# Attention values projected last and transposed one block at a time; attention operands fetched through GpSimd's DMA queue

## The chip, the cores and the metric

The kernel runs on one core of a Trainium2 chip. The core has five engines that run their own instruction streams in order: TensorE (PE in the profile), VectorE (DVE), ScalarE (ACT), GpSimd (POOL) and SyncE (SP, which only issues transfers here). They meet at semaphores. The metric is the device time of one execution in microseconds; less is better. The kernel before takes 1205.3 us as the median of three runs (1205.23 to 1207.03).

## The reference

One layer of a decoder with two token mixers beside each other, on 1024 tokens of width 1024 in float32. Cut to what matters:

```python
h = rmsnorm(x, norm_g)
proj = h @ w_in                       # 1024 x 9232, all projections at once
# four heads of gated linear attention (GLA), chunks of 64 tokens, a recurrent state per head
o_gla = gla_chunked(g_q, g_k, g_v, log_a)
y_a = (rmsnorm(o_gla, gla_norm_g) * silu(g_gate)) @ w_pa
# eight heads of stick-breaking attention, head width 128, blocks of 128 queries
z = q @ k.T * scale                   # strictly causal
A = exp(log_sigmoid(z) + (sum over s<j<t of log_sigmoid(-z)))
y_b = ((A @ v) * silu(s_gate)) @ w_pb
gates = sigmoid(m_logits + b_gate)
out = rmsnorm(x + (gates[0] * y_a + gates[1] * y_b) @ w_o, final_g)
```

## The kernel before, in words

**Precision.** Every large product is done in three passes: each float32 operand is split into a high part (an ACT copy into the matmul type, line 165) and a low part (a DVE subtraction, line 166), and high x high, high x low and low x high are added in PSUM. So each projected weight or operand costs ACT, DVE and PE work in step.

**The pairs.** Most projections are done two 128-column blocks at a time by a seven-product scheme (class Pairs, lines 62 to 99, and `pair_job`). A pair is seven units, u0 to u6; each unit is 12 matmuls of 128x512 (lines 270 to 272). Units 1, 4, 5 and 6 each finish one 128x512 block of the result, which is then evicted. While a unit of one pair runs, the weights of the next are split (lines 165 and 166), and GpSimd forms four weight differences per pair (lines 244 to 247). There are 28 pairs: three merge-gate pairs, the eight of GLA, the stick-breaking queries, values and keys in turn (four times query, value, key), four merge-gate pairs of the second branch, and one last merge-gate pair.

**The value pairs.** Queries and keys are evicted as they are. A value block is needed with tokens on the partitions, and as differences of neighbouring tokens. So the eviction of a value block copies the ends of its 128-token blocks into `vend` (line 605), forms the differences on DVE (lines 613, 615, 617), and appends a function `turn` to the list `late`: four PE transposes into a PSUM bank named tr (line 622), the split of that bank (lines 165 and 166), and two stores into `d_v` (line 626). `Pairs.run` takes the list as it stands before a unit and runs all of it behind that unit's product. Unit 5 leaves two functions there (its own block and the held one of unit 4), units 1 and 6 leave one each. There are two tr banks; GLA's transposes (lines 830 and 870) use the same two.

**GLA beside the pairs.** From about 280 us to 718 us the 32 GLA steps run, each with four units of the pairs between its parts. Its chain goes over PE, ACT, DVE, one small GpSimd power (line 231) and back. In this stretch the order on the engines is set by a scheduler, which places instructions by its own estimates.

**The attention.** From 737 us to about 1012 us the 64 stick-breaking steps run (8 heads x 8 blocks of 128 queries). A step is scores on PE (lines 966 to 968), a sigmoid on ACT (969), a scan on DVE (972), transposes on PE (984), and twice a head the product with the values (1005 to 1007). Between them stand filler units, 24 matmuls each (lines 204 to 206): first the attention's output gates, later the GLA branch's output projection, whose results are multiplied by a merge gate fetched from `d_ga` (line 590) and passed through a sigmoid (591). `load_head` fetches the keys (1 MB, line 909) and the two halves of the values (512 KB each, line 912) of a head; `load_q` fetches two query blocks (256 KB, line 919) into one of two buffers, which comes free when PE has used the queries before. All of it goes through SP's queue, as do every other load and nearly every store: an SP instruction whose buffer isn't free holds up all that stand behind it.

Of the kernel before, what the change touches and what calls it, by code (L numbers as in the profile page):

```python
# [9 lines left out]
F32 = mybir.dt.float32  # L10
# [14 lines left out]
DV = 256  # L25
# [5 lines left out]
C_SQ, C_SK, C_SV, C_SG, C_MA, C_MB = 3088, 4112, 5136, 6160, 7184, 8208  # L31
# [37 lines left out]
class Pairs:  # L69
# [13 lines left out]
    def run(self, n=None):  # L83
        while self.at < 7 * len(self.jobs) and (n is None or n > 0):
            i, u = divmod(self.at, 7)
            nxt = self.jobs[i + 1] if i + 1 < len(self.jobs) else None
            if u == 0:
                self.jobs[i]["split"][3]()
            elif nxt and u in (2, 4, 6):
                nxt["split"][u // 2 - 1]()  # L90
            if u == 1 and i + 2 < len(self.jobs):
                self.jobs[i + 2]["load"]()
            due = self.late[:]
            self.late.clear()
            self.jobs[i]["unit"](u)
            for f in due:
                f()
            self.at += 1
            if n is not None:
                n -= 1  # L100
# [3 lines left out]
def hybrid_layer(ctx: ExitStack, tc: tile.TileContext, x, norm_g, w_in, w_up, b_dec,  # L104
# [5 lines left out]
    nc = tc.nc  # L110
# [386 lines left out]
    f = {}  # L497
# [44 lines left out]
    def qk_pair(c0, i, dst):  # L542
        def evict(J, n, bank, add):
            v = total(bank, add)
            o = stage()
            split(v, o[:, 0], o[:, 1])
            nc.sync.dma_start(dst[2 * i + J][:, :, half(n)], o.bitcast(F32))

        return pair_job(w_in, c0 + i * DV, evict)
# [27 lines left out]
    def merge_pair(c0, i, dst):  # L577
        def evict(J, n, bank, add):
            if add is None:
                add = ev.tile([P, HALF], F32, tag="f", name="f")  # L580
                nc.scalar.activation(add, bank, AF.Copy)
            else:
                total(bank, add)
            nc.sync.dma_start(dst[2 * i + J][:, half(n)], add)

        return pair_job(w_in, c0 + i * DV, evict)
# [6 lines left out]
    def sv_pair(i):  # L593


        held = []

        def evict(J, n, bank, add):
            if add is None:
                add = ev.tile([P, HALF], F32, tag="f", name="f")  # L600
                nc.scalar.activation(add, bank, AF.Copy)
            else:
                total(bank, add)
            h = 2 * i + J
            nc.vector.tensor_copy(vend[:, h, 4 * n:4 * n + 4], add[:, P - 1:HALF:P])
            held.append((J, n, h, add))
            if (J, n) != (1, 1):
                while held:
                    diff(*held.pop())

        def diff(J, n, h, add):
            d = ev.tile([P, HALF], F32, tag="f", name="f")
            nc.vector.tensor_sub(d[:, 1:HALF], add[:, 0:HALF - 1], add[:, 1:HALF])
            if n:
                nc.vector.tensor_sub(d[:, 0:1], vend[:, h, 3:4], add[:, 0:1])
            else:
                nc.vector.tensor_scalar(d[:, 0:1], add[:, 0:1], -1.0, None, op0=ALU.mult)

            def turn():
                pt = ps.tile([P, HALF], F32, tag="tr", name="tr")  # L620
                for b in range(4):
                    nc.tensor.transpose(pt[:, b * P:(b + 1) * P], d[:, b * P:(b + 1) * P], ident)
                o = stage()
                split(pt, o[:, 0], o[:, 1])
                for e in range(2):
                    nc.sync.dma_start(d_v[h][:, 4 * n:4 * n + 4, e],
                                      o[:, e].bitcast(F32).rearrange("p (b c) -> p b c", c=P))

            late.append(turn)

        return pair_job(w_in, C_SV + i * DV, evict)

    def gla_qk(i):
# [5 lines left out]
    late = []  # L639
    pairs = Pairs([merge_pair(C_MA, i, d_ga) for i in range(3)] +  # L640
                  gla_qk(0) + [gg_pair(0), gg_pair(1)] + gla_qk(1) + [gg_pair(2), gg_pair(3)] +
                  [f for i in range(4) for f in (qk_pair(C_SQ, i, d_q), sv_pair(i), qk_pair(C_SK, i, d_k))] +
                  [merge_pair(C_MB, i, d_gb) for i in range(4)] + [merge_pair(C_MA, 3, d_ga)], late)

    dq_ctx = ExitStack()
    dq = dq_ctx.enter_context(tc.tile_pool(name="dq", bufs=1, reuse_waits="tile"))
# [259 lines left out]

    def load_head(h):
        kts[h] = sl.tile([P, 2, T], F32R, tag="k", name="k")
        nc.sync.dma_start(kts[h].bitcast(F32), d_k[h])
        vts[h] = [sl.tile([P, NT // 2, 2, P], F32R, tag="v", name="v", bufs=3) for _ in range(2)]  # L910
        for i, v in enumerate(vts[h]):
            nc.sync.dma_start(v.bitcast(F32), d_v[h][:, 4 * i:4 * i + 4])

    def load_q(h, m):

        tag = "d" + "hl"[m % 2]
        t = sw.tile([P, 4, P], F32R, tag=tag, name="q", bufs=1).rearrange("p a c -> p (a c)")
        t = t.rearrange("p (s c) -> p s c", s=2)
        nc.sync.dma_start(t.bitcast(F32), d_q[h][:, :, m * DV:(m + 1) * DV])
        for e in range(2):  # L920
            qts[h, 2 * m + e] = t[:, :, e * P:(e + 1) * P]

# [568 lines left out]
```

## Time and profile before

The profiled execution took 1206.26 us and its span is 1204.4 us; the three runs have a median of 1205.3 us.

| | busy us (share of the span) |
|---|---|
| PE (matmul) | 1184.0 (98%) |
| PEld (weight load) | 996.3 (83%) |
| DVE | 823.4 (68%) |
| ACT | 522.1 (43%) |
| POOL | 281.4 (23%) |

| stage, us from the span's start | what runs |
|---|---|
| 0 to 114 | norm, transposes of x, GLA values |
| 114 to 726 | the 28 pairs; GLA steps beside them from about 280 |
| 737 to 1012 | attention, with filler projections |
| 1044 to 1204 | output projections of the second branch, then the output |

Such a profile is read by the engine that is never idle: PE is busy in 98% of the span, at the full granted clock in all 40 slices of the page. An engine's idle time matters only where PE waits for it.

### The profile page before, as it was taken

The page shows a single profiled execution, that of the slowest core. Times are in us where ns is not written, and L with a number is a line of the kernel's source. Part 1 is how long each engine was busy: PE and PEld are TensorE (multiplying, and loading weights), DVE is VectorE, ACT ScalarE, POOL GpSimd, SP SyncE. Part 2 cuts the span into 40 slices and gives each one's busy share as a digit, 9 for nine tenths or more (in the row PEclk, how much of TensorE's full clock was granted, in tenths as well). Part 3 has the DMA queues.
Part 4 walks back from the last instruction along what each step waited for, and adds up shares of the span by engine and source line. Part 5 has one row for each costly group of instructions (what it writes and reads, how often), then busy time and mean ns, then how long its engine had stood idle before and what let it go on. Part 6 is the DMA issues. An engine that isn't in the chain of part 4 may idle for free.

```text
span 1204.4 us, 17022 instructions
## 1 busy us (share of the span) xinstructions
PE 1184.0 (98%) x6087; PEld 996.3 (83%) x6087; DVE 823.4 (68%) x1373; ACT 522.1 (43%) x985; POOL 281.4 (23%) x237
## 2 busy tenths in 40 slices
PE   8999999999999999999999999999999999999997
PEld 8999878788888887878788887888888888888886
DVE  6474877886777777766665544665675765578986
ACT  5343662333444444445443433343443443455543
POOL 1495523242424222322422300000000000800001
PEclk9999999999999999999999999999999999999999
DMA  7443449997556656656654359554689537748652
GB/s 282 193 152 130 149 168 304 324 328 241 163 161 186 220 177 201 205 179 201 206 175 141 126 184 294 187 192 156 235 282 314 176 123 249 253 163 287 219 192 105
DMA packets 192496, 247.65 MB, mean 206 GB/s; under 512 B 12406, under 2 KB 125068, under 8 KB 190876
## 3 DMA queue, kind: packets, MB, share of 16 engines
q1 hardware_dynamic: 191836, 245.52, 61.2%
q8 instruction: 48, 0.79, 0.3%
q10 hardware_dynamic: 576, 1.05, 0.2%
q14 instruction: 36, 0.29, 0.1%
HBM read 154.25 MB, written 92.27 MB: 205 GB/s over the span
## 4 chain that ended last, share of the span: by engine, by line
PE 85%; DVE 5%; DMA 3%; ACT 3%; issue 2%; POOL 1%; SPq 0%; ACTq 0%; DVEq 0%
PE pp L270 13%; PE pp L271 12%; PE pp L272 12%; PE pp L223 8%; PE pp L204 5%; PE pp L206 5%; PE pp L205 5%; PE z L966 2%; PE av L1006 1%; PE av L1007 1%; PE av L1005 1%; PE tr L984 1%; PE z L967 1%; PE z L968 1%; PE xb L1375 1%
## 5 line engine op out<-in xcount | busy, mean ns | idle before, releaser
L166 DVE TENSOR_TENSOR wl<-tt,wh 128x1024 fp32r<-128x1024 f32 x56 | 69.7, 1244 | 43.4 <-ACT wh L165 43.2
L972 DVE TENSOR_TENSOR_SCAN be<-be,m 128x128 f32<-128x128 f32 (+3 forms) x64 | 86.1, 1350 | 10.3 <-ACT be L969 10.0
L309 DVE TENSOR_TENSOR f<-pp,f 128x512 f32<-128x512 f32 x84 | 57.6, 686 | 51.1 <-PE pp L272 49.2
L244 POOL TENSOR_TENSOR tt<-raw 128x512 f32<-128x512 f32 x28 | 41.6, 1487 | 204.0 <-DVE wl L166 179.0
L166 DVE TENSOR_TENSOR wl<-raw,wh 128x1024 fp32r<-128x1024 f32 x47 | 65.2, 1389 | 31.3 <-ACT wh L165 30.7
L165 ACT ACTIVATE wh<-tt 128x1024 fp32r<-128x1024 f32 x56 | 59.2, 1058 | 61.7 <-PE pp L271 61.2
L165 ACT ACTIVATE wh<-raw 128x1024 fp32r<-128x1024 f32 x47 | 49.6, 1058 | 83.0 <-PE pp L205 41.3
L276 ACT ACTIVATE f<-pp 128x512 f32<-128x512 f32 x84 | 49.5, 591 | 71.3 <-PE pp L272 71.3
L1158 POOL TENSOR_TENSOR N<-A,A 128x512 f32<-128x512 f32 x4 | 6.6, 1649 | 304.0 <-DMA A<-d_osb 304.0
L231 POOL TENSOR_TENSOR r<-r,nhalf 128x1 f32<-128x1 f32 x40 | 24.7, 617 | 187.9 <-DVE r L230 177.4
L969 ACT ACTIVATE be<-z 128x384 f32<-128x384 f32 (+4 forms) x96 | 46.6, 494 | 49.8 <-PE z L968 48.7
L270 PE MATMUL pp<-ha22h,wh 128*128 128x512 f32 x112 | 44.5, 397 | 1.4 <-DVE f L309 1.4
L270 PE MATMUL pp<-S3h,wh 128*128 128x512 f32 x112 | 44.3, 395 | 1.5 <-ACT f L276 1.5
L270 PE MATMUL pp<-ha11h,wh 128*128 128x512 f32 x112 | 44.6, 398 | 0.0
L270 PE MATMUL pp<-S1h,wh 128*128 128x512 f32 x112 | 44.3, 396 | 0.0
L270 PE MATMUL pp<-ha12h,wh 128*128 128x512 f32 x112 | 44.2, 395 | 0.0
L270 PE MATMUL pp<-S2h,wh 128*128 128x512 f32 x112 | 44.0, 392 | 0.0
L270 PE MATMUL pp<-S4h,dh 128*128 128x512 f32 x112 | 43.9, 392 | 0.0
L272 PE MATMUL pp<-ha11h,wl 128*128 128x512 f32 x112 | 43.9, 392 | 0.0
L272 PE MATMUL pp<-ha12h,wl 128*128 128x512 f32 x112 | 43.7, 391 | 0.0
L272 PE MATMUL pp<-ha22h,wl 128*128 128x512 f32 x112 | 43.7, 390 | 0.0
L271 PE MATMUL pp<-ha22l,wh 128*128 128x512 f32 x112 | 43.7, 390 | 0.0
(519 smaller groups left out, 3902.6 us busy)
## 6 DMA issues: line engine op xcount, KB each, us to landing
raw<-in_w_in_dram SPq DMA_DIRECT2D x31, 1024.0 KB, 6.1
d_gv<-o SPq DMA_DIRECT2D x16, 512.0 KB, 2.6
d_t<-t SPq DMA_DIRECT2D x16, 512.0 KB, 5.8
v<-d_gv SPq DMA_DIRECT2D x32, 256.0 KB, 3.1
d_ogl<-o SPq DMA_DIRECT2D x64, 128.0 KB, 2.4
d_q<-o SPq DMA_DIRECT2D x16, 512.0 KB, 3.8
d_v<-o SPq DMA_DIRECT2D x32, 256.0 KB, 2.4
d_k<-o SPq DMA_DIRECT2D x16, 512.0 KB, 4.0
```

The lines of the kernel that those rows point to most:

```text
L165: nc.scalar.activation(hi, src, AF.Copy)
L166: eng.tensor_sub(lo, src, hi.bitcast(F32))
L204: nc.tensor.matmul(pt, whi[:, kb], h_, start=kb == 0, stop=False)
L205: nc.tensor.matmul(pt, whi[:, kb], l_, start=False, stop=False)
L206: nc.tensor.matmul(pt, wlo[:, kb], h_, start=False, stop=kb == KB - 1)
L223: nc.tensor.matmul(pt[:, 0:n], *ops[kb][i], start=k == 0, stop=k == 3 * KB - 1)
L270: nc.tensor.matmul(pt, bh[:, j], ah[:, j], start=first and j == 0, stop=False, skip_group_check=True)
L271: nc.tensor.matmul(pt, bh[:, j], al[:, j], start=False, stop=False, skip_group_check=True)
L272: nc.tensor.matmul(pt, bl[:, j], ah[:, j], start=False, stop=j == 3, skip_group_check=True)
L276: nc.scalar.activation(t[nm], t[bank], AF.Copy)
L309: nc.vector.tensor_add(add, bank, add)
L972: nc.vector.tensor_tensor_scan(rest, rest, m1[:, off:T][:, ::-1], 1.0, op0=ALU.mult, op1=ALU.max)
```

## The change

Three things. First, `Pairs.run` takes one function of `late` per unit and leaves the rest for the units behind it, where it took all. Second, the four value pairs no longer stand between the query and key pairs: queries and keys alternate, then come the four merge-gate pairs, then the four value pairs in a row, then the last merge-gate pair. Third, the loads of keys, values and queries of the attention are issued by GpSimd, not by SP.

```diff
@@ Pairs.run
-            due = self.late[:]
-            self.late.clear()
+            due = self.late.pop(0) if self.late else None
             self.jobs[i]["unit"](u)
-            for f in due:
-                f()
+            if due:
+                due()
@@ the list of pairs
-                  [f for i in range(4) for f in (qk_pair(C_SQ, i, d_q), sv_pair(i), qk_pair(C_SK, i, d_k))] +
-                  [merge_pair(C_MB, i, d_gb) for i in range(4)] + [merge_pair(C_MA, 3, d_ga)], late)
+                  [f for i in range(4) for f in (qk_pair(C_SQ, i, d_q), qk_pair(C_SK, i, d_k))] +
+                  [merge_pair(C_MB, i, d_gb) for i in range(4)] +
+                  [sv_pair(i) for i in range(4)] + [merge_pair(C_MA, 3, d_ga)], late)
@@ load_head, load_q
-        nc.sync.dma_start(kts[h].bitcast(F32), d_k[h])
+        nc.gpsimd.dma_start(kts[h].bitcast(F32), d_k[h])
...
-            nc.sync.dma_start(v.bitcast(F32), d_v[h][:, 4 * i:4 * i + 4])
+            nc.gpsimd.dma_start(v.bitcast(F32), d_v[h][:, 4 * i:4 * i + 4])
...
-        nc.sync.dma_start(t.bitcast(F32), d_q[h][:, :, m * DV:(m + 1) * DV])
+        nc.gpsimd.dma_start(t.bitcast(F32), d_q[h][:, :, m * DV:(m + 1) * DV])
```

Lines 97 to 640 of the kernel before have numbers lower by one in the changed kernel (622 becomes 621), so the rows below differ in these numbers too.

**DVE at the end of a value pair.** Before, here the second value pair (o<-tr,o is the low half of a turned block, vend and f<-f its differences):

```order
L613 TENSOR_TENSOR f<-f 128x511
L615 TENSOR_TENSOR f<-vend,f 128x1
L166 TENSOR_TENSOR wl<-tt,wh 128x1024
L605 COPY vend<-f 128x4
L613 TENSOR_TENSOR f<-f 128x511
L615 TENSOR_TENSOR f<-vend,f 128x1
L166 TENSOR_TENSOR o<-tr,o 128x512 x3
L309 TENSOR_TENSOR f<-pp,f 128x512
```

Changed, between the first and the second value pair:

```order
L612 TENSOR_TENSOR f<-f 128x511
L614 TENSOR_TENSOR f<-vend,f 128x1
L165 TENSOR_TENSOR o<-tr,o 128x512 x2
L308 TENSOR_TENSOR f<-pp,f 128x512
...
L604 COPY vend<-f 128x4
L612 TENSOR_TENSOR f<-f 128x511
L616 TENSOR_SCALAR f<-f 128x1
L165 TENSOR_TENSOR o<-tr,o 128x512
```

Three low halves in a row have become two, and the third stands behind the first eviction of the next pair, which is a value pair as well and brings its own copy and differences with it.

**SP where the second half of the filler projections begins** (oa22l is the last of the GLA results fetched, d_ga a merge gate, v and q values and queries, d_osb and d_ma results). Before:

```order
L1077 DMA oa22l<-d_ogl_141 128x4x512
L912 DMA v<-d_v_97 128x1024
L590 DMA o<-d_ga_142 128x512
L919 DMA q<-d_q_81 128x2x256
L1012 DMA d_osb_112<-f 128x512
L912 DMA v<-d_v_98 128x1024
L919 DMA q<-d_q_81 128x2x256
L1052 DMA d_ma_158<-o 128x512
L590 DMA o<-d_ga_143 128x512
```

Changed:

```order
L1077 DMA oa22l<-d_ogl_141 128x4x512
L589 DMA o<-d_ga_142 128x512
L589 DMA o<-d_ga_143 128x512
L589 DMA o<-d_ga_144 128x512
L1012 DMA d_osb_112<-f 128x512
```

The first merge gate stands directly behind oa22l, and the second and third follow it.

**PE at the start of the attention**, the rows ahead of the scores of the fifth query block (z 128x320, which needs the third query load; tr<-ident,be is a turned block, pp a filler). Before:

```order
L204 MATMUL pp<-ha11h,wh 128x512
L205 MATMUL pp<-ha11l,wh 128x512
L206 MATMUL pp<-ha11h,wl 128x512
L984 MATMUL tr<-ident,be 128x128 x3
L204 MATMUL pp<-ha12h,wh 128x512
L205 MATMUL pp<-ha12l,wh 128x512
L206 MATMUL pp<-ha12h,wl 128x512
L204 MATMUL pp<-ha11h,wh 128x512
L205 MATMUL pp<-ha11l,wh 128x512
L966 MATMUL z<-k,q 128x320
```

Changed:

```order
L967 MATMUL z<-k,q 128x512
L968 MATMUL z<-k,q 128x512
L204 MATMUL pp<-ha12l,wh 128x512
L984 MATMUL tr<-ident,be 128x128
L205 MATMUL pp<-ha12h,wl 128x512
L984 MATMUL tr<-ident,be 128x128 x2
L966 MATMUL z<-k,q 128x320
```

Between the scores of the second block and these scores stood 14 fillers and 6 transposes; now there are 6 fillers and 3 transposes, and the others stand behind. On POOL, which has no other work from 722 us on but for the loads, this third query load stands behind the clearing of the buffers for the scan, the second head's keys and the first half of its values.

## The prediction

> **What bounds the kernel now.** I read the engines' busy time first, then what PE waited for, then each wait in order of time. The page's first row and the waits of PE (line, releaser: us in total, times, longest):
>
> ```profile
> PE 1184.0 (98%) x6087; PEld 996.3 (83%) x6087; DVE 823.4 (68%) x1373; ACT 522.1 (43%) x985; POOL 281.4 (23%) x237
> PE tr L622 <- DVE o L166: 2.1, 2, 1.1
> PE z L966 <- ACT be L969: 1.3, 1, 1.3
> PE tr L622 <- DVE f L617: 0.9, 2, 0.6
> PE tr L870 <- DVE o L166: 0.8, 1, 0.8
> PE tr L984 <- DVE atl L166: 0.7, 1, 0.7
> PE z L966 <- DMA q<-d_q: 0.2, 1, 0.2
> ```
>
> PE sets the time, and the change takes no matmul away. So it can win only the idle time of PE in the stages that it touches, and these six rows are all of it: 2.1 + 1.3 + 0.9 + 0.8 + 0.7 + 0.2 = 6.0 us. The same waits in the timeline of PE (start, duration, instruction, idle time before it and its releaser):
>
> ```profile
> 439.17 0.66 PE L622 MATMUL tr<-ident,f 128*128 128x128 f32 x4 [0.58 <-DVE f L617]
> 457.33 0.66 PE L622 MATMUL tr<-ident,f 128*128 128x128 f32 x4 [1.02 <-DVE o L166]
> 527.00 0.66 PE L622 MATMUL tr<-ident,f 128*128 128x128 f32 x4 [1.06 <-DVE o L166]
> 597.07 0.44 PE L870 MATMUL tr<-ident,on 128*128 128x128 f32 x2 [0.81 <-DVE o L166]
> 742.58 0.55 PE L984 MATMUL tr<-ident,be 128*128 128x128 f32 x3 [0.70 <-DVE atl L166]
> 744.46 0.41 PE L966 MATMUL z<-k,q 128*128 128x320 f32 x1 [0.18 <-DMA q<-d_q]
> 926.18 0.38 PE L966 MATMUL z<-k,q 128*128 128x256 f32 x1 [1.26 <-ACT be L969]
> ```
>
> Three groups: the turned value blocks (439 to 597), the start of the attention (742 to 744), and one wait for ACT in its middle (926).
>
> **Part 1, one block per product.** The waits at 457, 527 and 597 (2.9 us) are for "DVE o", the low half taken from a tr bank. There are two such banks. A 128x512 matmul takes PE 0.23 us, as a row of the chain of waits has it:
>
> ```profile
> 737.93 0.23 PE pp L204
> ```
>
> Before, two blocks are turned behind unit 6 and a third behind unit 0 of the next pair, so the third needs a bank that was filled only one unit earlier. Now it is the third unit in a row with one block each, and the bank it needs was filled two units earlier. That is one more product, about 2.7 us (12 matmuls), against a longest wait of 1.06. I count all 2.9 us as gone. The two waits for "DVE f L617" (0.9 us) stand behind unit 2, where the first block of a pair is turned one unit after its difference, before and now; I keep them. Bounds for this part without the next one: -3.8 to 0.
>
> **Part 2, value pairs in a row.** The work is the same, but DVE's load is no longer mixed. Windows of one pair each, a value pair and two merge-gate pairs (length, PE, PEld, DVE, ACT, POOL busy, granted clock, DMA share, GB/s), and what a value pair alone asks of DVE, the groups of all four (busy us, mean ns):
>
> ```profile
> 428.35:453.29 24.94, 24.36 (x129) 19.94 (x128) 18.81 (x44) 10.75 (x24) 6.43 (x6) 1.00 0.54 166
> 639.83:662.73 22.90, 22.90 (x118) 18.89 (x116) 12.66 (x32) 9.28 (x22) 6.17 (x6) 1.00 0.43 137
> 662.73:685.43 22.70, 22.70 (x116) 18.71 (x114) 12.01 (x25) 9.43 (x18) 5.86 (x6) 1.00 0.42 136
> L613 DVE TENSOR_TENSOR f<-f 128x511 f32<-128x511 f32 x16 | 10.8, 681 | 0.0
> L166 DVE TENSOR_TENSOR o<-tr,o 128x512 fp32r<-128x512 f32 x16 | 10.6, 679 | 1.4 <-ACT o L165 1.4
> L605 DVE COPY vend<-f 128x4 f32<-128x4 f32 x16 | 4.5, 281 | 0.2
> L615 DVE TENSOR_TENSOR f<-vend,f 128x1 f32<-128x1 f32 x8 | 4.5, 559 | 0.0
> L617 DVE TENSOR_SCALAR f<-f 128x1 f32<-128x1 f32 x8 | 1.2, 144 | 0.0
> 370.45 0.44 PE tr L622 x4
> ```
>
> A merge-gate pair has 12.3 us of DVE in 22.8 us. A value pair adds 31.6 / 4 = 7.9 us of DVE, and 4 x 0.44 = 1.8 us of PE: in a row, DVE is busy 20.2 of 24.6 us, 82%. Before, a third of that spilled into a key pair. As long as DVE may idle less than 4.4 us in such a pair, PE hides it: cost 0. If it can't, this cover is gone, and PE waits for differences and banks (rival D). GpSimd's and SP's work per pair is the same.
>
> **Part 3, loads through GpSimd.** Nothing is saved on the DMA engines; what moves is which queue a late load holds up. Two places count.
>
> At 908 us SP fetches the first merge gate. The rows of SP, then of ACT, then of what ACT waited for in all:
>
> ```profile
> 900.42 1.06 SPq L1077 DMA_DIRECT2D oa22l<-d_ogl  x1
> 908.26 0.33 SPq L912 DMA_DIRECT2D v<-d_v  x1
> 908.64 0.42 SPq L590 DMA_DIRECT2D o<-d_ga  x1
> 914.00 0.72 ACT L591 ACTIVATE o<-o,vcol 128x512 f32<-128x512 f32 x1 [2.09 <-DMA o<-d_ga]
> 924.93 0.72 ACT L591 ACTIVATE o<-o,vcol 128x512 f32<-128x512 f32 x1 [2.06 <-DMA o<-d_ga]
> 925.55 1.06 ACT L969 ACTIVATE be<-z 128x512 f32<-128x512 f32 x2
> ACT o L591 <- DMA o<-d_ga: 34.8, 11, 10.9
> ```
>
> SP stood from 901.5 to 908.26 at a value load whose buffer wasn't free, with the merge gate behind it. It landed late, ACT stood 2.09 us, the result's store and with it the reuse of the buffers came late, ACT stood 2.06 us once more at 924.93, and the sigmoid behind it (925.55) is what PE waits for at 926.18. Now the load stands directly behind oa22l, 6.7 us earlier. Its chain moves up by ACT's first wait, 2.09 us, more than PE's 1.26: -1.3. The other bound is 0, if a later merge gate, which still waits for a store, is late instead.
>
> At the start of the attention the third query load has the shortest time between the release of its buffer and its use. Rows of PE, SP and the chain of waits, and the landing of all 32 query loads:
>
> ```profile
> 737.65 0.28 PE L968 MATMUL z<-k,q 128*128 128x256 f32 x1
> 738.65 0.32 SPq L571 DMA_DIRECT2D d_sg<-o  x1
> 739.08 0.52 SPq L919 DMA_DIRECT2D q<-d_q  x1
> 739.08 5.34 DMA q<-d_q
> L919 SPq DMA_DIRECT2D q<-d_q x32: 523/524/878, 728.2 to 979.7; - x32
> DMA to landing us min/median/max: 2.9/4.4/7.3
> ```
>
> The buffer is free at 737.65 + 0.28 = 737.9; SP, busy with a store, issued at 739.1. GpSimd has nothing to do there and issues about 738.1. But PE's order changed too: the scores that need this load have moved ahead of 8 fillers and 3 transposes. PE was ready for them at 744.46 - 0.18 = 744.3; without 8 x 0.23 and 3 x 0.11 us and without the wait of 0.70 at 742.58 it is ready at 744.3 - 2.9 = 741.4. The load lands between 738.1 + 2.9 = 741.0 and 738.1 + 7.3 = 745.4. I take the duration that this very load had, 5.34, since no row shows a load through GpSimd: 743.4, so PE waits 2.0 us where it waited 0.70 + 0.18: +1.1. Bounds -0.9 to +3.1. In the notes called the Trainium skill, the page "DMA: Bandwidth & Descriptors" (Latency and other measured facts) gives a first byte after about 1 us for loads through GpSimd and 0.6 us through SP or ACT; by it, this term would be an estimated +1.5 and the total 0.4 us more. No run shows that yet.
>
> The other loads have more time. Released by the scores of the fourth block and used by those of the seventh, the next load has, from 739.41 + 0.40 to 749.28, 9.5 us, above the longest landing of 7.3:
>
> ```profile
> 739.41 0.40 PE L968 MATMUL z<-k,q 128*128 128x512 f32 x1
> 749.28 0.45 PE L966 MATMUL z<-k,q 128*128 128x448 f32 x1
> ```
>
> **Sum.** -2.9 + 0 - 1.3 + 1.1 = -3.1 us. The profiled execution (1206.26 us, 1.9 more than its span of 1204.4) would take 1203.2; it lies 1.0 above the median, so the median becomes 1205.3 - 3.1 = 1202.2.
>
> **Rivals.**
>
> A, all of it goes: the waits behind unit 2 vanish in the even spacing, and the third query load lands in 2.9 us, before PE asks. For it: each wait is at most 1.3 us. Against: unit 2 hasn't changed. All 6.0 us: 1199.3.
>
> B, the third query load lands in 7.3 us, the longest seen: PE waits 4.0 us there, +3.1 net. -2.9 - 1.3 + 3.1 = -1.1: 1204.2. For it: second keys and first values stand ahead of it in the same queue.
>
> C, the waits for banks form again, since every pair brings its blocks upon the last one's: part 1 yields nothing. -1.3 + 1.1: 1205.1.
>
> D, DVE becomes the bound in the row of value pairs. In the window 428.35 it idled 24.94 - 18.81 = 6.1 us, in its order behind ACT, GpSimd and PE. If that much can't be avoided, a pair takes 20.2 + 6.1 = 26.3 us instead of 24.6; four of them cost 6.9, and part 1 is lost: 1205.3 + 6.9 - 1.3 + 1.1 = 1212.0, slower. It decides from 4.4 us of forced idle time. Against: DVE idles there also because it is ahead.
>
> E, GpSimd's queue is slow throughout. From a landing of 9.5 us on, each head waits at least once. At 12 us: the third load costs 738.1 + 12 - 741.4 - 0.9 = 7.8, eight heads 8 x 2.5 = 20, and -2.9 - 1.3: 1228.9. For it speaks no row. A rule of the Trainium skill does, "SBUF — State Buffer" (SBUF: two separate sides): descriptors from GpSimd wait while a two-port DVE operation runs. No run shows it yet.
>
> That the change doesn't do what it says is excluded by the order of the rows.
>
> **How the numbers follow.** A difference under about 0.2%, 2.4 us, can't be told from no change here: faster is below 1202.9, slower above 1207.7. Forecast 0.57 (its own range 1200.4 to 1204.5; 0.42 of it faster, 0.15 within), A 0.10, B 0.12, C 0.09, D 0.08, E 0.04. Faster 0.42 + 0.10 = 0.52; within 0.15 + 0.12 + 0.09 = 0.36; slower 0.08 + 0.04 = 0.12. The range 1199.6 to 1206.2 holds the forecast, B, C and part of A, and leaves out D and E.
>
> **What would show it.** Right: no waits of PE for "DVE o" at the turned blocks; a wait of about 2 us for q at the first scores of 320 columns; ACT's waits for d_ga well below 34.8 us and none of PE at the scores behind them. Wrong: waits at the turned blocks between 600 and 710 us that sum to more than 1 us; windows of value pairs longer than 25 us; PE waits for q in later heads; query loads that land above 7.3 us.

## The result, and the profile after

The changed kernel takes 1218.1 us (median of 4 runs, 1217.1 to 1221.0) against 1205.3 (4 runs, 1204.1 to 1207.0): 1.0109 times the time before, 95% interval 1.0088 to 1.0131. It is 12.9 us slower where 3.1 us faster was forecast. The profiled execution took 1217.6 us, its span is 1215.9, 11.5 longer than before. One execution of the experiment e_sp below took 1465.0 us at a granted clock of 0.752; it is a slow one, and neither it nor its profile is used.

The page's row of busy time and the waits of PE in the changed kernel (line, releaser: us in total, times, longest):

```profile
PE 1185.2 (97%) x6087; PEld 998.1 (82%) x6087; DVE 824.9 (68%) x1373; ACT 521.2 (43%) x985; POOL 318.1 (26%) x293
PE z L966 <- ACT be L969: 13.8, 4, 7.7
PE tr L621 <- DVE f L616: 0.9, 1, 0.9
PE pp L204 <- DMA ha21l<-d_a: 0.6, 1, 0.6
PE av L1006 <- DVE atl L165: 0.4, 1, 0.4
```

The waits for "DVE o" at the turned blocks are gone, and PE is busy 1.2 us more than before. What is new is one row: scores that wait for the sigmoid ahead of them, 13.8 us. They stand in the timeline of PE at four places:

```profile
736.11 0.44 PE L966 MATMUL z<-k,q 128*128 128x384 f32 x1 [2.04 <-ACT be L969]
917.89 0.47 PE L966 MATMUL z<-k,q 128*128 128x448 f32 x1 [2.62 <-ACT be L969]
925.31 0.50 PE L966 MATMUL z<-k,q 128*128 128x512 f32 x1 [1.44 <-ACT be L969]
957.09 0.69 PE L966 MATMUL z<-k,q 128*128 128x384 f32 x1 [7.71 <-ACT be L969]
```

How far ahead of the kernel before was PE? The attention has 16 value products. The start of the first matmul of each, read off PE's timeline, minus the same in the kernel before (us; negative is ahead):

| value product | 1 | 9 | 10 | 11 | 12 | 13 | 16 |
|---|---|---|---|---|---|---|---|
| before, started at | 751.0 | 886.6 | 905.2 | 920.7 | 940.1 | 956.0 | 1006.4 |
| changed kernel | -4.0 | -4.0 | -4.0 | -0.6 | +1.2 | +10.6 | +10.6 |

So PE came 4.0 us ahead into the attention and lost 14.6 us between 901 and 967 us: in the attention nothing before that stretch and nothing after it (a last 0.9 us is lost behind the attention).

Not all of the 4.0 us is the change's doing. The first matmul of the first GLA step (pa<-q,ke) starts at 284.6 before and at 282.5 here, 2.1 us ahead, and up to there the two kernels do the same work; two waits at 225 and 232 us, for the eviction of a pair's block, were 1.54 and 1.26 us before and nothing and 0.97 here. From that matmul to the first value product PE took 466.5 us before and 464.6 in the changed kernel: 1.9 us are gained where the change acts.

The waits in the stretch from 901 to 967 us are 2.62 + 0.40 + 1.44 + 7.71 = 12.2 us. The rest is clock, as far as it can be estimated. Windows of 4 us (length, PE, PEld, DVE, ACT, POOL busy, granted clock, DMA share, GB/s):

```profile
912.00:916.00 4.00, 3.28 (x17) 2.52 (x15) 0.00 (x0) 0.00 (x0) 0.00 (x0) 1.00 1.04 408
916.00:920.00 4.00, 2.11 (x11) 1.97 (x12) 2.44 (x3) 3.19 (x6) 0.00 (x0) 0.91 0.90 307
920.00:924.00 4.00, 3.47 (x14) 2.55 (x13) 1.19 (x3) 0.00 (x0) 0.00 (x0) 0.66 0.58 193
952.00:956.00 4.00, 0.00 (x0) 0.00 (x0) 0.00 (x0) 0.01 (x1) 0.00 (x0) 0.68 0.50 184
956.00:960.00 4.00, 2.91 (x8) 2.53 (x9) 2.93 (x3) 2.29 (x5) 0.73 (x1) 0.50 0.00 0
```

After the stands of 2.62 and 7.71 us PE is granted less of its clock for some us. As an estimate, busy time times the missing share, 2.11 x 0.09 + 3.47 x 0.34 + 2.91 x 0.50, is 2.8 us; 12.2 + 2.8 = 15.0, about the 14.6 lost. From 912 to 916 neither DVE nor ACT did anything while the DMA engines were full, and PE ran out of work at 915.3.

What ACT waited for, its rows say (its own order; the idle time before each in brackets):

```profile
916.74 0.72 ACT L590 ACTIVATE o<-o,vcol 128x512 f32<-128x512 f32 x1 [7.86 <-DMA o<-d_ga]
917.37 0.85 ACT L969 ACTIVATE be<-z 128x384 f32<-128x384 f32 x2
942.99 0.72 ACT L590 ACTIVATE o<-o,vcol 128x512 f32<-128x512 f32 x1 [6.86 <-DMA o<-d_ga]
955.99 0.72 ACT L590 ACTIVATE o<-o,vcol 128x512 f32<-128x512 f32 x1 [7.75 <-DMA o<-d_ga]
956.62 0.42 ACT L969 ACTIVATE be<-z 128x320 f32<-128x320 f32 x1
```

The sigmoid of a merge gate stands in ACT's order ahead of the sigmoid of a score. When its d_ga load is late, the score behind it is late too, and PE with it. ACT waited 56.7 us for d_ga in all, against 34.8 before. Why the first of these loads is late is in the rows of SP, then of GpSimd:

```profile
887.80 0.32 SPq L1012 DMA_DIRECT2D d_osb<-f  x1
895.61 0.32 SPq L995 DMA_DIRECT2D f<-d_sg  x1
896.03 0.39 SPq L1077 DMA_DIRECT2D oa21l<-d_ogl  x1
900.39 7.12 SPq L589 DMA_DIRECT2D o<-d_ga  x3
```

```profile
887.51 0.58 POOL L909 DMA_DIRECT2D k<-d_k  x1
904.66 0.58 POOL L912 DMA_DIRECT2D v<-d_v  x1 [9.56 <-PE av L1007]
906.49 0.55 POOL L912 DMA_DIRECT2D v<-d_v  x1 [1.26 <-PE av L1007]
```

Two things meet. SP stood from 888 to 895.6 at a gate load of the values (L995), whose buffer is that of the d_osb store just issued; the store took 7.8 us, beside a 1 MB key load on GpSimd's queue. So the four 1 MB reloads (oa21l to oa22l) went out at 896.0, no earlier than the 895.9 of before, though PE was 4 us ahead, and the d_ga loads followed behind them. Then two value loads came on GpSimd's queue. The queues in 910 to 915 us, of the changed kernel and of the one before (packets, MB, share of the 16 engines):

```profile
q0 software_dynamic: 349, 1.18, 57.9%
q1 hardware_dynamic: 457, 0.88, 45.5%
```

```profile
q1 hardware_dynamic: 816, 1.62, 93.9%
```

GpSimd's queue (q0) took more than half of the engines just when SP's queue (q1) held what ACT needed.

The longest stand, 7.71 us, is the same once more. SP stood from 929.9 to 936.2 behind the next d_osb store, and sent the load of the merge gate that ACT ran at 942.99 only at 940.3. Behind that sigmoid stood the split of a weight block, and behind the split the next weight load (945.95) and the next d_ga load:

```profile
946.39 0.57 SPq L589 DMA_DIRECT2D o<-d_ga  x1
```

Two value loads went out on GpSimd's queue at 944.7 and 946.6, and ACT had this merge gate at 955.99, 9.6 us after the issue of its load.

Over the kernel the landings of the d_ga loads (us, min/median/max) went from the first of these rows, before, to the second, after: the median fell, the longest doubled. The first load, issued at 900.4, has no landing in the trace; ACT's wait for it ended at 916.7.

```profile
DMA to landing us min/median/max: 2.5/5.2/6.7
```

```profile
DMA to landing us min/median/max: 2.5/3.8/13.8
```

### The profile page after: what moved, and what is told of

It reads as the page before. It is cut to its first block, busy times and chain, and to the rows that moved or that the text cites. A ratio compares the mean times of both kernels' runs of the same rounds, so it can differ in the third digit from the quotient of the medians.

```text
span 1215.9 us, 17082 instructions
## 1 busy us (share of the span) xinstructions
PE 1185.2 (97%) x6087; PEld 998.1 (82%) x6087; DVE 824.9 (68%) x1373; ACT 521.2 (43%) x985; POOL 318.1 (26%) x293
## 4 chain that ended last, share of the span: by engine, by line
PE 82%; DMA 7%; DVE 5%; ACT 3%; issue 2%; SPq 1%; POOL 0%; ACTq 0%; DVEq 0%
PE pp L269 13%; PE pp L271 13%; PE pp L270 13%; PE pp L222 8%; PE pp L204 3%; PE pp L205 3%; PE pp L203 3%; DMA o<-d_ga 2%; PE z L966 1%; DMA d_ma<-o 1%; PE z L968 1%; PE z L967 1%; DMA raw<-in_w_in_dram 1%; PE tr L984 1%; PE xb L1374 1%
## 5 line engine op out<-in xcount | busy, mean ns | idle before, releaser
L919 POOL DMA_DIRECT2D q<-d_q x32 | 23.0, 720 | 176.2 <-PE tr L984 91.8
L966 PE MATMUL z<-k,q 128*128 128x384 f32 (+4 forms) x96 | 38.3, 399 | 13.9 <-ACT be L969 13.8
L270 PE MATMUL pp<-S2l,wh 128*128 128x512 f32 x112 | 43.7, 390 | 0.0
```

Of the source, the lines that this page charges most:

```text
L270: nc.tensor.matmul(pt, bh[:, j], al[:, j], start=False, stop=False, skip_group_check=True)
L966: nc.tensor.matmul(zt[:, 0:n], q[:, 0], k[:, 0, ksl], start=True, stop=False)
```

## The experiments

Two theories came out of these rows. **Theory S**, share: bytes of keys and values on a second queue take the engines from the loads that are needed next, while on SP's one queue they came in their turn. **Theory O**, order: SP, no longer held at the key and value loads, runs ahead and stands at another place, the gate load behind the store. Times below are medians; ratios are against the kernel before run beside them.

### Which part, and which loads

All are the changed kernel with some loads put back on SP, but for e_pool, which is the kernel before with all three on GpSimd's queue.

```diff
 e_sp (k, v, q back), e_q (k, v back), e_kv (q back), e_k (v, q back), e_v (k, q back)
-        nc.gpsimd.dma_start(kts[h].bitcast(F32), d_k[h])
+        nc.sync.dma_start(kts[h].bitcast(F32), d_k[h])
```

> The changed kernel with the query, key and value loads of the attention put back on SP's queue: parts 1 and 2 alone. Theory T (part 3 loses the time: in the profile of the changed kernel the value loads on GpSimd's queue take 57.9% of the DMA engines in 910 to 915 us, the d_ga loads behind the four 1 MB reloads on SP's queue land at 916.7, ScalarE stands 7.9, 6.9 and 7.8 us on them in its own order, and TensorE stands 12.1 us in all behind it and is then granted 0.50 to 0.91 of its clock for some us): without part 3 the lead of some 4 to 7 us with which the changed kernel reaches the attention is kept: 1198.5 to 1202.5. Rival R1 (the stalls come from the lead itself: an attention that starts 7 us earlier meets d_ga loads that come no earlier): the lead is eaten wherever the loads are issued, 1204 to 1212.

> The kernel before with part 3 alone: query, key and value loads of the attention on GpSimd's queue, value pairs and turned blocks as they were. Theory T: the queue alone makes the stalls on the late d_ga loads, so slower than before by at least half of what the changed kernel lost from its lead (it was some 6.6 us ahead at the attention and ended 11.5 behind in the profiled span, so some 18): 1213 to 1224. Rival R1: without the lead of parts 1 and 2 the loads are in time, 1204 to 1208.

> The changed kernel with the key and value loads back on SP, only the query loads on GpSimd's queue. Theory T with the 512 KB value loads as what pushes the d_ga loads back: close to the kernel without part 3, 1198.5 to 1203.5. Rival R2 (not the share of the DMA engines, but SP's new order without the query loads between its gate and merge loads): the stalls stay, 1209 to 1219.

> The changed kernel with the query loads back on SP, key and value loads on GpSimd's queue. Theory T with the value loads as what pushes the d_ga loads back: most of the loss stays, 1209 to 1219. Rival R2 (SP's order without the query loads): the query loads stand between the gate and merge loads again and the loss goes, 1199 to 1205.

> The changed kernel with queries and keys back on SP, only the value loads on GpSimd's queue. Two places are late in the profile of the changed kernel: at 887.5 a key load runs beside the store of d_osb (landing 7.8 us), behind which SP stands with the next gate load until 895.6; and at 904 to 915 two value loads take over half of the engines while the d_ga loads, queued behind four 1 MB reloads, land 10.7 and 13.8 us after issue. Theory Tv (the value loads decide): with them on GpSimd's queue the loss stays, 1210 to 1220. Theory Tk (the key load beside the store decides, since all that follows is queued behind it): 1200 to 1204.

> The changed kernel with queries and values back on SP, only the key loads on GpSimd's queue. Theory Tv (the value loads beside the reloads decide): 1199.5 to 1204. Theory Tk (the key load beside the store of d_osb decides): 1210 to 1220.

| kernel | on GpSimd's queue | us | ratio to before (95%) |
|---|---|---|---|
| e_sp: parts 1 and 2 | none | 1201.5 | 0.997 (0.9959 to 0.9981) |
| e_q | q | 1201.3 | 0.997 (0.9961 to 0.9979) |
| e_k | k | 1210.0 | 1.0026 (1.0008 to 1.0043) |
| e_v | v | 1211.9 | 1.0036 (1.0018 to 1.0054) |
| e_kv | k, v | 1218.6 | 1.0109 (1.0094 to 1.0125) |
| changed kernel | k, v, q | 1218.1 | 1.0109 (1.0088 to 1.0131) |
| e_pool: part 3 alone | k, v, q | 1217.8 | 1.0094 (1.0066 to 1.0122) |

Parts 1 and 2 alone are about 4 us faster. All the loss is from part 3, and in it from keys and values; the 32 query loads cost nothing. That the lead of parts 1 and 2 made the loss itself (rival R1) falls with e_sp and e_pool. R2, that the query loads missing from SP's order make it, falls with e_q. Keys alone cost 8.7 us over e_q and values alone 10.6 (6.7 and 8.0 by the ratios), so neither "the values decide" nor "the key decides" holds: e_v fits the first of these theories and e_k, at the edge of its range, the second. The kernels with keys or values on GpSimd's queue also scatter: e_pool from 1210.6 to 1222.6, e_k from 1205.5 to 1216.3, while all but one of the 11 runs of e_q lie within 2.1 us.

With q back on SP beside keys and values on the other queue, another load is the late one. PE's waits in e_kv, and then in e_k:

```profile
PE z L966 <- DMA q<-d_q: 8.1, 2, 4.8
PE z L966 <- ACT be L969: 2.7, 2, 2.4
```

```profile
PE z L966 <- DMA q<-d_q: 6.5, 4, 2.8
```

So it isn't d_ga as such: whatever stands in SP's queue and is needed next.

### Parts 1 and 2 apart

```diff
 e_one (loads on SP, pair order of before)
+                  [f for i in range(4) for f in (qk_pair(C_SQ, i, d_q), sv_pair(i), qk_pair(C_SK, i, d_k))] +
 e_ord (loads on SP, all due blocks at once, as before)
+            due = self.late[:]
+            self.late.clear()
```

> Part 1 alone: one turned block behind each product, the value pairs between the query and key pairs as before, all loads on SP. The terms of the prediction: three waits of TensorE on the copies of turned blocks go, 2.9 us, so 1202.0 to 1203.5. Rival: the blocks of the value pairs now come up behind products of the key pairs and part 2 is needed for the gain, which is then shared: 1204 to 1206. The two parts together with the loads on SP measured 1201.53.

> Part 2 alone: the four value pairs behind the query and key pairs, all turned blocks that are due behind one product as before, all loads on SP. The terms of the prediction: value pairs in a row cost nothing and the waits on turned blocks stay, 1205 to 1206. Rival: most of the 4.0 us that both parts together gained comes from the new order of the pairs, which puts the wait-free query and key pairs together: 1202 to 1204; a second rival is the bound of VectorE in the value row with bursts of turned blocks, over 1207.

Part 1 alone measured 1204.0 (ratio 0.9978, 0.9969 to 0.9988), part 2 alone 1204.5 (0.9984, 0.9973 to 0.9995), with a before of 1205.9 beside them; both together 1201.5, with 1205.6. So neither is 0; e_one is at the edge of its rival's range, e_ord between its two. The intervals overlap each other and that of both together, so the times alone don't divide the gain. The profiles do it better: from the first GLA matmul (pa<-q,ke) to the first value product PE took 466.5 us before, 464.4 in e_one, 464.8 in e_ord, and 462.9 with both (e_q). That is 2.1 and 1.7 for the parts and 3.6 for both. The waits say where. PE in e_one, and then in e_ord:

```profile
PE tr L829 <- DVE o L165: 1.0, 1, 1.0
PE tr L869 <- DVE o L165: 1.0, 1, 1.0
PE tr L621 <- DVE f L616: 0.9, 2, 0.6
```

```profile
PE tr L622 <- DVE o L166: 1.0, 1, 1.0
PE tr L622 <- DVE f L617: 0.9, 1, 0.9
PE tr L871 <- DVE o L166: 0.8, 1, 0.8
```

Each part alone leaves two of the waits for "DVE o", at other places; with both there is none. In e_one both are at GLA's own transposes (lines 829 and 869), which use the same banks: part 1 spreads the blocks, and among GLA steps they still meet these. So each part has a share of its own; nothing here shows that they need each other.

### Share or order

e_stub lets SP issue a small first piece of each key and value load, so that it waits for the freed buffers in its turn; the rest goes on GpSimd's queue. e_g3 gives the gates three buffers of their own, e_stubg does both, and e_small cuts the loads into pieces of 1 KB per row.

```diff
 e_stub
-        nc.gpsimd.dma_start(kts[h].bitcast(F32), d_k[h])
+        for eng, c in ((nc.sync, slice(0, 16)), (nc.gpsimd, slice(16, T))):
+            eng.dma_start(kts[h][:, :, c].bitcast(F32), d_k[h][:, :, c])
 (values: block 0 of four on SP, 1 to 3 on GpSimd's queue)
 e_g3
-        gate = ev.tile([P, HALF], F32, tag="f", name="f")
+        gate = sb.tile([P, HALF], F32, tag="fg", name="fg", bufs=3)
 e_small
+        for s in range(2):
+            for c in range(0, T, 256):
+                nc.gpsimd.dma_start(kts[h][:, s, c:c + 256].bitcast(F32), d_k[h][:, s, c:c + 256])
```

> The changed kernel with a small first piece of each key load (16 of 1024 columns) and of each value load (one of four blocks) back on SP, the rest on GpSimd's queue: SP again waits for the freed buffers in its turn, but nearly all key bytes and three quarters of the value bytes still travel on the second queue. Theory S (the second queue takes its share of the engines from the loads that are needed next): near the changed kernel, 1211 to 1219. Theory O (SP, no longer held at the key and value loads, runs ahead and gets stuck at other places): near the kernel with keys and values on SP, 1201 to 1205.

> The changed kernel with three buffers of their own for the gates of the values, so that the gate load (L995) on SP does not wait for the store of d_osb. In the profile of the changed kernel SP stood there until 895.6, and the four 1 MB reloads and the d_ga loads came behind. Theory O (SP stuck at that place): the reloads start some 5 to 8 us earlier, most of the loss goes, 1201 to 1208. Theory S (share of the engines): the d_ga loads stay late, 1212 to 1220.

> Both edits together: small first pieces of keys and values on SP and three gate buffers. SP is then paced as in the kernel with keys and values on SP and is not stuck at the gate load; what is left of the change is that most key and value bytes travel on the second queue. Theory S: still 1209 to 1219. Theory O: 1200.5 to 1204.

> The changed kernel with the key and value loads cut into pieces of 1 KB per partition row (eight loads for a head's keys, four for each half of the values), all on GpSimd's queue; the orders of SP and ScalarE are unchanged. In the profile of the changed kernel the second queue's packets averaged 4.2 KB (25.17 MB in 6016) against about 1.2 KB on SP's queue. Theory S, with a share that goes by packets: the second queue takes less, the d_ga loads land earlier, 1204 to 1213. Theory S with a share by bytes, or theory O: as the changed kernel, 1215 to 1221.

Measured: e_stub 1209.6, e_g3 1214.5, e_stubg 1209.2, e_small 1209.3. e_stub lies between the ranges of both theories. e_g3 is a failed experiment: SP's waits in it, here from 880 to 985 us, show that with three buffers the gate load still waits for the buffer of the store just issued. So is e_stubg as a test of theory O, for the same reason (24.0 us in five such waits in the same stretch).

```profile
SPq L995 <- DMA d_osb<-fg: 30.4, 5, 8.2
```

e_small took 8.8 us off, and its rows of SP show two effects at once: GpSimd's queue had 43.8% of the engines in 910 to 915 (57.9% in the changed kernel), and the store, issued at 888.52, let SP go on at 892.58 instead of after 7.8 us.

```profile
888.52 0.32 SPq L1015 DMA_DIRECT2D d_osb<-f  x1
892.58 0.32 SPq L998 DMA_DIRECT2D f<-d_sg  x1
```

To take the stand away for good, the product of values and gate goes to a tile of its own, from which d_osb is stored; the gate's buffer is then free when the multiplication is done.

```diff
 e_sep; e_sepstub = e_sep + e_stub; e_sepsmall = e_sep + e_small; e_sepq = e_sep + keys and values on SP
-        gate = ev.tile([P, HALF], F32, tag="f", name="f")
+        gate = sb.tile([P, HALF], F32, tag="fg", name="fg", bufs=3)
+        res = ev.tile([P, HALF], F32, tag="f", name="f")
-            nc.vector.scalar_tensor_tensor(gate[:, cs], pav[:, cs], vend[...], gate[:, cs],
+            nc.vector.scalar_tensor_tensor(res[:, cs], pav[:, cs], vend[...], gate[:, cs],
-        nc.sync.dma_start(d_osb[h][:, half(g)], gate)
+        nc.sync.dma_start(d_osb[h][:, half(g)], res)
```

> The changed kernel with the products of values and gate written to a tile of their own, from which d_osb is stored, and three gate buffers: the gate load on SP now waits only for the multiplication, not for the store ahead of it. (In the run with three gate buffers alone that wait stayed: SP L995 stood 30.4 us in five waits on the stores of d_osb, since each gate load takes the buffer of the store just issued; so that run said nothing of theory O.) Theory O (SP stuck at that place makes the reloads and the d_ga loads late): 1201 to 1208. Theory S (share of the engines): 1212 to 1220. Both by halves: 1208 to 1213.

> The same separate product tile, with small first pieces of the key and value loads on SP, the rest on GpSimd's queue: SP has the same order, and waits for the same buffers, as in the kernel with the separate product tile and keys and values on SP (run beside it); what differs is that most key and value bytes travel on the second queue. Theory S: 5 to 12 us slower than that kernel, 1206 to 1214. Theory O: within 2 us of it, 1200 to 1204.

> The separate product tile with keys and values on SP, queries on GpSimd's queue: the control of the run before, and a candidate to beat both kernels. No theory sees a wait of TensorE on SP's gate load there: as the kernel without the separate tile, 1200 to 1203.

> The separate product tile with all key and value loads on GpSimd's queue in pieces of 1 KB per row. If the loss is the sum of a share of the engines that goes by packets (small pieces alone took 8.8 us off) and of SP stuck at the gate load (theory O), both are now taken away: 1200 to 1205. If theory O has no part in it: 1207 to 1212.

The last run is the other way round: e_q, with a stand put in.

```diff
 e_qwait (ahead of the second set of reloads)
+                if n and not e:
+                    nc.sync.dma_start(oq[n, e][1][:, 0, 0:16].bitcast(F32), d_osb[4][:, 0:16])
```

> The fast kernel (keys and values on SP, queries on GpSimd's queue, 1201.3) with one wait put in: ahead of the second set of 1 MB reloads a load of 16 columns from the d_osb block whose store has just been issued, so that SP stands there until that store has landed (some 6.5 us after its issue at 887.3, and for one reload the 2 us more that the small load takes). The bytes of keys and values stay on SP. Theory O alone is enough: the reloads start 2 to 5 us later, the d_ga loads behind them too, 1204 to 1210. Theory O needs the second queue's share beside it (only with key and value bytes out of SP's order are the loads behind the reloads late enough): 1200.5 to 1203.

| keys and values | SP free to go on | SP stands at the store, about 888 us |
|---|---|---|
| on SP | e_q 1201.3, e_sepq 1201.9 | e_qwait 1204.4 |
| on the second queue, small first pieces on SP | e_sepstub 1208.1 | e_stub 1209.6, e_stubg 1209.2 |
| wholly on the second queue | e_sep 1206.9 | changed kernel 1218.1, e_g3 1214.5, e_kv 1218.6 |

The ratios to before: e_sepq 0.9963 (0.9950 to 0.9976), e_qwait 0.9994 (0.9985 to 1.0004), e_sep 1.0007 (0.9994 to 1.0020), e_sepstub 1.0015 (1.0004 to 1.0026). e_qwait and e_sep lie in the range expected by theory O, e_sepstub in that of theory S; e_sepsmall missed the 1200 to 1205 that theory O and a share by packets together gave. Both theories have a part in the loss, and they don't make the whole.

**The stand.** Put into e_q alone, with the order of PE, ACT, DVE and GpSimd unchanged, it costs 3.1 us (theory O). Taken out of the changed kernel (e_sep), with one sigmoid at another place in ACT's order, it gives 11.2 back. Between e_sepstub and e_stub (1.0033, 1.0015 to 1.0052), whose PE, ACT and DVE run in the same order, it is worth 1.4, and their intervals overlap. The rows of SP in e_qwait, in e_sep and in e_stub, around the same place:

```profile
887.84 0.32 SPq L1012 DMA_DIRECT2D d_osb<-f  x1
894.03 0.32 SPq L1077 DMA_DIRECT2D oa21l<-d_osb  x1
```

```profile
889.26 0.32 SPq L1013 DMA_DIRECT2D d_osb<-f  x1
889.67 0.38 SPq L996 DMA_DIRECT2D fg<-d_sg  x1
893.45 0.37 SPq L1078 DMA_DIRECT2D oa21l<-d_ogl  x1
```

```profile
889.00 0.32 SPq L1014 DMA_DIRECT2D d_osb<-f  x1
895.18 0.32 SPq L997 DMA_DIRECT2D f<-d_sg  x1
```

In e_qwait SP stood 5.9 us, in e_stub as long; in e_sep it went on at once.

**The second queue.** Without a stand it costs 6.2 us between e_sepq and e_sepstub, 5.0 between e_sepq and e_sep. This isn't theory S alone. SP has nearly the same order in e_sepq and e_sepstub (not quite, as the expectation has it: some neighbours change places at the start of the attention and around the value loads), but ACT's order differs too, in e_sepstub as in the changed kernel. In e_q and e_sepq ACT runs both sigmoids of 384 columns, and later both of 320 columns, before the next merge gate. This is e_q:

```profile
908.34 1.06 ACT L969 ACTIVATE be<-z 128x384 f32<-128x384 f32 x2
909.29 0.71 ACT L590 ACTIVATE o<-o,vcol 128x512 f32<-128x512 f32 x1
```

In the changed kernel the gate stands ahead of both sigmoids of 384 columns (916.74 above) and between the two of 320 (955.99 above), and PE's stands of 2.62 and 7.71 us follow just there; in e_sepstub it stands between the two of each kind, and 2.5 of the 4.7 us that PE waited between 900 and 960 us follow the gate between the two of 320. No run has ACT's order of e_q with keys and values on the second queue, so how much of the 5 to 6 us is the share of the engines and how much the order on ACT stays open. ACT's order alone doesn't make the long stands: e_small has on ACT the very order of the changed kernel, and PE waited 3.2 us for sigmoids in all, not 13.8. The share in one window doesn't settle it either: in e_sep GpSimd's queue had 61.2% of the engines in 910 to 915 us, more than in the changed kernel.

**What is more than the sum.** Stand and second queue together cost 16.8 us in the changed kernel, but with small first pieces on SP (e_stub) 8.3, less than 3.1 + 6.2. So the excess comes only with SP freed of the key and value loads. In the changed kernel SP sent the first merge gate's load at 900.4; in e_stub at 905.9, behind the first piece of a value load, as in e_q (904.2). The first gate's sigmoid ran as late in e_stub (916.8), but one sigmoid of 384 columns stood ahead of it, and PE waited 0.9 us there and 2.6 at the later place, where the changed kernel waited 2.6 and 7.7. Which of the two, SP's pace or ACT's order, does it wasn't measured apart.

**Small pieces.** On every engine the order of e_sepsmall is that of e_sep, but for the number of pieces, and small pieces bring nothing more there: e_sepsmall takes 1207.9 (1.0012, 1.0000 to 1.0024). That points to the store that landed earlier as what they brought in e_small; a lower share of the second queue alone didn't show in the time. It isn't settled further: e_sepsmall's waits are small ones for query loads (4.5 us in four), other than e_sepstub's.

No run beats e_q and e_sp, 1201.3 and 1201.5: both beat the kernel before by 0.3%. Moving the query loads adds nothing that can be measured.

## Why the prediction was wrong

**Part 1 and part 2: right in direction and nearly in size, not in the split.** The forecast was -2.9 and 0, together; e_sp and e_q measured -4.0 and -4.3 in the medians. The three waits are gone, one wait for "DVE f" of 0.9 stays, as kept. PE's waits from 280 to 1020 us in e_q:

```profile
PE tr L621 <- DVE f L616: 0.9, 1, 0.9
PE z L966 <- DMA q<-d_q: 0.7, 1, 0.7
PE av L1006 <- DVE atl L165: 0.2, 1, 0.2
```

That is 1.8 us where the kernel before had 6.0. What is gained beside the 2.9 is mostly the wait for ACT at 926 (1.3): the prediction booked it on part 3, and it went with keys and values still on SP. The whole gain of these parts was booked on part 1; the profiles of e_one and e_ord give 2.1 to it and 1.7 to part 2. DVE has room in the value pairs; three windows among them in the changed kernel (columns as above):

```profile
602.41:626.93 24.52, 23.61 (x123) 19.15 (x121) 18.05 (x42) 10.02 (x23) 6.43 (x6) 1.00 0.43 132
626.93:651.94 25.01, 25.01 (x135) 20.44 (x134) 18.09 (x43) 11.46 (x26) 6.94 (x6) 1.00 0.51 160
651.94:676.64 24.70, 24.70 (x134) 20.48 (x133) 18.93 (x47) 11.73 (x24) 6.26 (x6) 1.00 0.61 172
```

DVE is busy 18.1 to 18.9 us where 20.2 were worked out, and PE stands 0.9 us in all. One window is 25.01 us long, at the edge of the 25 named as a sign against the forecast, but PE is busy throughout it. Rivals C and D are out.

**Part 3, the third query load: the right kind of wait, too large, and covered.** In the changed kernel PE waited for no query load. It stood 2.04 us just ahead, at the scores of 384 columns, for ACT, which waited for a weight load:

```profile
734.35 1.06 ACT L164 ACTIVATE wh<-raw 128x1024 fp32r<-128x1024 f32 x1 [7.63 <-DMA raw<-in_w_in_dram]
```

In e_q, without that stand, PE did wait for the query load at the scores of 320 columns: 0.7 us, where 2.0 was forecast. The query loads landed after 3.0/4.2/8.4 us (min/median/max) through GpSimd's queue in the changed kernel and 3.4/5.8/8.0 in e_q, 2.9/4.4/7.3 through SP's before: in both some landed above the 7.3 that I named as a sign against me. The Trainium skill gives a later first byte for GpSimd loads ("DMA: Bandwidth & Descriptors", Latency and other measured facts). These medians neither bear that out nor exclude it, since one is below that of before and one above. The Trainium skill's rule that descriptors from GpSimd wait behind two-port DVE work ("SBUF — State Buffer", SBUF: two separate sides) isn't tested by any run here. Rival E is out: e_q waited for one query load, and not for one in each head. That its time, like D's, lay in the right direction is luck.

**Part 3, the first merge gate: the step that failed.** "Now the load stands directly behind oa22l, 6.7 us earlier. Its chain moves up": the load was issued at 900.4, 8.2 us earlier than before. But ACT could use it only at 916.7, 16.4 us after its issue, where it had taken 5.4 before (908.6 to 914.0). The prediction carried the short time of the old place over to the new one. At the old place SP, held at the value load until 908, had sent nothing for 6.8 us while the reloads drained. That was the work of the very thing that I counted as an obstacle. Freed of it, the d_ga loads queue behind 4 MB of reloads, and the value loads, now on a queue of their own, come in beside them. The first sigmoid ran 2.7 us later than before, for a PE that was 4 us earlier. The prediction also took ACT's order to stay as it was. In the changed kernel the later gate stands between the two sigmoids of 320 columns, where it stood behind both before, and the longest stand, 7.71 us, is at that place. The bounds of the term, -1.3 to 0, held no loss at all: the upper one, a later merge gate that is late instead, took the wait of before as the worst case. In the trace the stretch from 901 to 967 us cost 14.6 us; taking keys and values off the second queue gives 16.8 back (1218.1 less 1201.3).

**"Nothing is saved on the DMA engines; what moves is which queue a late load holds up"** was the right sentence, read in one direction only. I asked which loads are no longer held up and not which ones lose their turn. At 901 to 912 us the DMA share was 1.02 before and 1.04 after, so the engines were full both times; there a transfer that comes in early makes another late. In the Trainium skill "DMA: Bandwidth & Descriptors" (Issuing engines are not separate DMA queues) says that transfers of all issuing engines run on the same 16 DMA engines and interleave, and that a second issuing engine saves only time of the sequencer. The trace agrees with the first (57.9% and 45.5% in the same 5 us). On the second the runs go further: keys and values on the second queue cost 5.0 to 6.2 us even without a stand of SP, ACT's changed order included. I didn't weigh it.

**The range.** 1199.6 to 1206.2 was built from terms whose upper ends came from landings seen on one queue. The cases slower than before had 0.12, and none of them was this mechanism.

## What to carry to other kernels

In this kernel the single DMA queue, with loads that wait for their buffers, was also a pacer: it kept the loads behind them from crowding the engines. Before moving loads to a second queue, look at the stretch in which the DMA share is 1.0 and list what is needed next there; move only loads that are small or early (the query loads here), not the megabytes that would come in beside an urgent load. And where an engine works in order, ask for each load that may become late what else stands behind it on that engine: here a 256 KB merge gate stopped the scores by standing ahead of them on ACT. Compare that order between the two kernels too; here it changed when the loads moved.

## What the runs showed of the hardware

- The granted clock of TensorE fell after a stand of some us even in a kernel that is 97% busy: to 0.50 in the window after the stand of 7.7 us, and to 0.66 in a window that begins 2 us after the end of the stand of 2.6. In windows of 1 us it was 1.00 again at 961 and at 923 us, 4 and 5 us after the stands. By the estimate above this made stands of 12.2 us cost 15, where 14.6 were lost. In e_stub a stand of 2.56 us that ended at 953.7 left the clock at 1.00. The Trainium skill's "TensorE: Matmul & The Clock Gate" (What's actually happening) gives half the clock after an idle window of about 3.4 us; the 0.50 after 7.7 us agrees with it, the fall after 2.6 us doesn't follow from it.
- With two queues at work from 910 to 915 us, GpSimd's had 57.9% of the DMA engines for 1.18 MB in 349 packets, and SP's 45.5% for 0.88 MB in 457. With key and value loads in pieces of 1 KB per row (e_small) GpSimd's had 43.8%, 0.88 MB in 327 packets. That the size of the pieces makes this difference is not shown, since the order of the loads in these 5 us differs too.
- GpSimd issued a load in about 0.72 us for queries and 0.58 for keys, SP before in 0.52 and 0.60.
